# First modulation rows ahead of x, the first norm in wide tiles, and the order of the first products

## The chip, the cores and the metric

The kernel runs on one core of a Trainium2 chip (trn2). The metric is device time in microseconds (us), the median over runs of the same program. Engines are called TensorE (PE in the profile; PEld are its weight loads), VectorE (DVE), ScalarE (ACT), GpSimd (POOL) and SyncE (SP); SP issues most of the loads.

## The reference

One inference step of a two-layer diffusion backbone, all float32, for 512 latent and 128 prompt tokens of width 1024. What matters here is the beginning of layer 0:

```
def rms_norm(x, g):
    y = xf * lax.rsqrt(jnp.mean(xf * xf, axis=-1, keepdims=True) + RMS_EPS)
    return (y * g)

def ada_modulation(cond, w_mod, b_mod):
    m = jax.nn.silu(cond) @ w_mod + b_mod
    return jnp.split(m, 6, axis=-1)
...
        sh1_s, sc1_s, g1_s, sh2_s, sc2_s, g2_s = ada_modulation(cond_lat, w_mod[l], b_mod[l])
        hp = modulate(rms_norm(xp, norm_mix[l]), sh1_p, sc1_p)     # h * (1 + scale) + shift
        hs = modulate(rms_norm(xs, norm_mix[l]), sh1_s, sc1_s)
        # even layer: p = h @ w_in, split into latent attention, rotary key, neighbourhood attention
```

After it come two kinds of attention, output projection, a SwiGLU feed-forward layer, and layer 1 with grouped-query attention and its own feed-forward layer. The change touches only the first modulation, the first norm and the first projection.

## The kernel before

Activations lie with features on the 128 partitions: x is eight tiles `x[k]` of 128 features by 640 tokens, of which the first 512 are latent and the last 128 prompt tokens. Tokens are handled in two halves of 320 (`HALF`). Every float32 product is made of three: both operands are split into a high and a low part (`hh`, `hl` for activations, `unit` for weights: ScalarE makes the high part at L173, VectorE the low one at L174), and `mm3` issues high-high, high-low and low-high.

`Norm.add` (L201) squares a half tile on ScalarE and adds it to `acc` on VectorE; `Norm.rstd` (L211) sums over partitions with a product by ones on TensorE, and makes the reciprocal root with Ln and Exp on ScalarE, a half at a time (`n00p`, `n00rs` in the profile). `Mod.make` (L228) turns one half tile of x into `hh` and `hl`: VectorE multiplies by norm and scale (`h00t`, L234), ScalarE adds the shift (`h00h`, L238), VectorE makes the low part (`h00l`, L239). The second half has two conditions, so each step of it is two instructions (192 and 128 columns): a tile takes six on VectorE.

`mod0(j)` computes shift and scale for tiles 2j and 2j+1. Its two parts, called the rows of j, are 16 products of 32x256 each over one 1 MB load (`mraw`, fetched by `fetch`); ScalarE copies the sum out (`modsb`, L349), and `end` turns it with four small products by `sel`, and VectorE adds the bias (`mods`, L357). `mkgs` makes the scale column (`gs`, L364).

The stage is written out by hand. SP's queue issues x, the first rows' loads, wA0, the second rows' loads, wA1 and wA4, then the third and fourth rows' loads. `run(pieces)` has each piece begin after the last TensorE instruction issued before it, so TensorE's order is the written one; inside the pieces and on the other engines a planner orders the instructions, and each engine runs its own list in order. `first(ks, us)` issues the products of the activation tiles `ks` with the weight units `us`: unit 0 is wA0, units 1 and 2 are wA1 and wA4; two tiles and one unit are 12 products, with both other units 24. `made(j)` ends the modulation of j and makes tiles 2j and 2j+1. The order before is: the norm, rows 0, made(0), rows 1, 12 products of tiles 0 and 1 with wA0, made(1), 24 products with wA1 and wA4, rows 2, and so on with tiles 2 to 7. Behind the stage stand the products with wA2 and wA3 (`ckv0a`, from 53.3 us), and the rest of the kernel, whose text is the same in both versions.

Of the kernel before, what the change touches and what calls it, by code (L numbers as in the profile page):

```python
# [11 lines left out]
F32 = mybir.dt.float32  # L12
F32R = mybir.dt.float32r
AF = mybir.ActivationFunctionType
# [4 lines left out]
P = 128  # L19
D = 1024  # L20
KT = D // P
NS = 512
NP = 128
T = NS + NP
# [14 lines left out]
SH1, SC1, G1, SH2, SC2, G2 = 0, 8, 16, 24, 32, 40  # L39
# [12 lines left out]
def body(ctx, tc, xT, vecs, crow, wm0, wm0g1, wm0g, wm1, wA, wNV, wNA, wMK, wMV, wOA, wGQ, wGK, wGV, wOC,  # L52
         wFI, wFO, wFO1, cckvT, ckrT, cnkT, cnv, cgkT, cgv, rpbp, tabM, tabK, tabG, maskN,
         yT, o_ckvT, o_krT, o_nkT, o_nv, o_gkT, o_gv):
    nc = tc.nc
    V, S, G = nc.vector, nc.scalar, nc.gpsimd

    class PE:

        last = None  # L60
# [10 lines left out]
    ring = ctx.enter_context(tc.tile_pool(name="ring", bufs=8))  # L71
# [17 lines left out]
    def bank(name, kind="m"):  # L89
        if kind == "m":  # L90
            return psp.tile([P, 512], F32, tag="m", bufs=4, name=name)
        return ypool["pool"].tile([P, 512], F32, tag=kind, bufs=ypool["tags"][kind], name=name)
# [4 lines left out]
    def pair(name, kind="y"):  # L97
        return [bank(f"{name}a", kind), bank(f"{name}b", kind)]
# [7 lines left out]
    def f(ap):  # L106
        return ap.bitcast(F32)
# [4 lines left out]
    HALF = ((0, HT), (HT, T))  # L112
    HCOND = (((0, HT, 0),), ((HT, NS, 0), (NS, T, 1)))

    def run(pieces):

        for piece in pieces:
            with tc.issue_after(PE.last.ins):
                piece()
# [26 lines left out]
    mods = [main.tile([P, 48, 2], F32, name=f"mods{l}") for l in range(2)]  # L146
    gs = [[main.tile([P, 8, 2], F32, name=f"gs{l}{i}") for i in range(2)] for l in range(2)]
# [7 lines left out]
    def bc2(ap):  # L155
        return bass.AP(tensor=ap.tensor, offset=ap.offset, ap=list(ap.ap) + [[0, 2]])
# [6 lines left out]
    def load(src, n, name):  # L163
        raw = rawp.tile([P, 1024], F32, tag="raw", name=name)
        nc.sync.dma_start(raw[:, :n], src)
        return raw[:, :n]

    def unit(src, n, name, lo="v", pool=None, bufs=3):

        raw = load(src, n, name + "r")  # L170
        t = (pool or wp).tile([P, 2, 1024], F32R, tag="w", bufs=bufs, name=name)
        hi, lw = t[:, 0, :n], t[:, 1, :n]
        S.activation(hi, raw, AF.Copy)  # L173
        (V if lo == "v" else G).tensor_tensor(lw, raw, f(hi), ALU.subtract)  # L174
        return hi, lw
# [7 lines left out]
    def mm3(ps, a, b, h, l, st, sp, **k):  # L183
        PE.matmul(ps, a, h, start=st, stop=False, **k)
        PE.matmul(ps, a, l, start=False, stop=False, **k)
        PE.matmul(ps, b, h, start=False, stop=sp, **k)

    def proj(ps, wh, wl, hh, hl, ks, c0, c1, first=True, last=True, w0=0):

        for j, k in enumerate(ks):  # L190
            a, b = wh[:, (w0 + j) * P:(w0 + j + 1) * P], wl[:, (w0 + j) * P:(w0 + j + 1) * P]
            mm3(ps[:, :c1 - c0], a, b, hh[k][:, c0:c1], hl[k][:, c0:c1], first and j == 0, last and j == len(ks) - 1)


    class Norm:
# [5 lines left out]
        def add(self, x, i):  # L201
            c0, c1 = HALF[i]
            if self.k[i] == 0:
                S.activation(self.acc[:, c0:c1], x[:, c0:c1], AF.Square)
            else:
                sq = tp.tile([P, HT], F32, tag="u", bufs=7, name=f"{self.name}sq{self.k[i]}{i}")
                S.activation(sq, x[:, c0:c1], AF.Square)
                V.tensor_add(self.acc[:, c0:c1], self.acc[:, c0:c1], sq)
            self.k[i] += 1

        def rstd(self, i):  # L211
            c0, c1 = HALF[i]
# [118 lines left out]
    def mod0(j, bk, load_):  # L331

        box = []

        def part(half):
            def run():
                if half == 0:
                    box.append(bk())
                psm, rs = box[0], load_(j, half)

                for g in range(4):
                    for b in range(2):
                        o = 512 * (g % 2) + 256 * b
                        rows = slice(64 * b + 32 * (g % 2), 64 * b + 32 * (g % 2) + 32)
                        PE.matmul(psm[rows, :256], scol[:, 4 * half + g, :], rs[g // 2][:, o:o + 256], start=half == 0 and g < 2,
                                  stop=half == 1 and g > 1, tile_position=(0, rows.start))
                if half == 1:
                    box.append(tp.tile([P, HT], F32, tag="u", bufs=7, name=f"modsb{j}"))
                    S.activation(box[1][:, :256], psm[:, :256], AF.Copy)  # L349
            return run  # L350

        def end():
            psm, sb = box
            for i in range(2):
                PE.matmul(psm[:, 4 * i:4 * i + 4], sb[:, i * P:(i + 1) * P], sel, start=True, stop=True)
            for i, t in enumerate(MOD0[j]):
                V.tensor_tensor(mods[0][:, t:t + 2, :], psm[:, 0:8].rearrange("p (a i b) -> p a i b", a=2, b=2)[:, :, i, :],  # L357
                                bc2(bmod(0, t, 2)), ALU.add)
        return [part(0), part(1), end]

    def mkgs(l, i, k0=0, k1=8):
        sc = SC1 if i == 0 else SC2
        n = (V_NMIX if i == 0 else V_NFFN) + 8 * l
        V.scalar_tensor_tensor(gs[l][i][:, k0:k1, :], mods[l][:, sc + k0:sc + k1, :], 1.0, bc2(vec[:, n + k0:n + k1]),  # L364
                               ALU.add, ALU.mult)
# [111 lines left out]
        return get  # L477


    nrm = Norm("n00", D)  # L480
    x = []
    for k in range(KT):
        xk = ring.tile([P, T], F32, tag="x", name=f"x0_{k}")
        nc.sync.dma_start(xk, xT[:, k, :])
        x.append(xk)
    for k in range(KT):
        for i in range(2):
            nrm.add(x[k], i)
    hm = Mod("h00", x, gs[0][0], mods[0], SH1, (range(8), range(8)))
    hh, hl = hm.hh, hm.hl  # L490
    pss = [pair(f"wA{u}") for u in range(2)] + [[bank(f"wA2{c}") for c in range(2)]]

    def first(ks, us):
        for k in ks:
            for u in us:
                for c, (c0, c1) in enumerate(HALF):
                    proj(pss[u][c], *w3[u], hh, hl, [k], c0, c1, first=k == 0, last=k == KT - 1, w0=k)

    with tc.tile_pool(name="start", bufs=1) as big:
        raws = {}  # L500

        def fetch(j):
            for half in range(2):
                raws[j, half] = big.tile([P, 2, 1024], F32, tag="mraw", bufs=8, name=f"mraw{j}_{half}")
                nc.sync.dma_start(raws[j, half], wm0[j, 2 * half:2 * half + 2].rearrange("q p n -> p q n"))


        fetch(0)
        w3 = [unit(wA[0], 1024, "wA0")]
        fetch(1)  # L510
        w3 += [unit(wA[i], 1024, f"wA{i}") for i in (1, 4)]
        fetch(2)
        fetch(3)
        m = [mod0(j, lambda j=j: bank(f"mod{j}", "m"), lambda j, half: [raws[j, half][:, q, :] for q in range(2)]) for j in range(4)]

        def made(j):

            m[j][2]()
            mkgs(0, 0, 2 * j, 2 * j + 2)
            for k in (2 * j, 2 * j + 1):  # L520
                for i in range(2):
                    hm.make(i, nrm.rs, k)

        def rows(j):
            return m[j][:2]

        nrm.rstd(0)
        run([lambda: nrm.rstd(1)] + rows(0))
        run([lambda: made(0)] + rows(1))
        run([lambda: first((0, 1), [0]), lambda: made(1), lambda: first((0, 1), [1, 2])])  # L530
        run(rows(2))
        run([lambda: first((2, 3), [0]), lambda: made(2), lambda: first((2, 3), [1, 2])])
        run(rows(3))
        run([lambda: first((4, 5), [0]), lambda: made(3), lambda: first((4, 5), [1, 2])])
        run([lambda u=u: first((6, 7), [u]) for u in range(3)])
    sb = ExitStack()
# [53 lines left out]
    pss = [pair(f"ckv{u}") for u in range(2)]  # L590
# [15 lines left out]
    for kk in range(4):  # L606
# [3 lines left out]
        for j in range(2):  # L610
            k = 2 * kk + j
            a, b = wh[:, 512 * j:512 * (j + 1)], wl[:, 512 * j:512 * (j + 1)]
            for i in range(5):
                c0, c1 = P * i, P * i + P
# [256 lines left out]
    for h in range(8):  # L871
# [9 lines left out]
        qh, ql, ks = [t[r] for t in nqk[p]]  # L881
# [771 lines left out]
    x, pend = mixer_out(wOA, oMs + oNs, [4, 5, 6, 7, 0, 1, 2, 3], x_again, mods[0], "oa", nxt, op[-1], before(op[1], op[5], (1, 1, 1, 1, 0, 0, 0)))  # L1653
    box2, nxt = next_mod("h10", gs[1][0], mods[1], SH1)
    x, pend = ffn(0, x, pend, box["m"], nxt, side, op)


    hh, hl = box2["m"].hh, box2["m"].hl
# [17 lines left out]
    pss = [pair(f"gk{v}") for v in range(2)]  # L1676
# [165 lines left out]
    for h in range(8):  # L1842
# [4 lines left out]
        if h < 7:  # L1847
# [13 lines left out]
    x, pend = mixer_out(wOC, oGs, list(range(8)), lambda n, x=x: x[n], mods[1], "oc", nxt, op[-1],  # L1861
                        before(op[5], op[5], (2, 1, 1, 2, 1, 1, 0)), True)
# [9 lines left out]
    x, pend = ffn(1, x, pend, box["m"], final, lambda pool: lambda kind, i: None, op)  # L1872
# [158 lines left out]
```

## Time and profile before

| | |
|---|---|
| median of 3 runs | 1502.68 us (1501.55 to 1503.84) |
| the profiled execution | 1505.78 us |
| its span in the profile | 1503.8 us |
| TensorE busy, share of the span | 1449.1 us, 96% |
| VectorE, ScalarE, GpSimd busy | 82%, 52%, 12% |
| chain that ended last: TensorE, VectorE, DMA, ScalarE | 76%, 10%, 6%, 5% |
| loads from HBM | 193.15 MB |

The profile is one execution. The page cuts the span in 40 equal slices and gives each engine's busy share in tenths. A line of a timeline has start, length, engine, source line, operation, output <- inputs, shapes, and in brackets the idle time before it and what ended that. Several instructions of one kind are merged into one line (x4), whose length runs from the first start to the last end. For a load the last number of its line is the time from issue to landing.

### The profile page before, as it was taken

How to read it: one execution, taken by the hardware profiler on the slowest of the kernel's cores; microseconds unless marked ns; L12 is line 12 of the kernel's file. 1: busy time of each engine (PE TensorE's matmuls, PEld its weight loads, DVE VectorE, ACT ScalarE, POOL GpSimd, SP SyncE). 2: the span in 40 equal slices, each digit the busy share in tenths (PEclk: the TensorE clock that was granted, in tenths of full speed). 3: DMA queues.
4: the chain of work that ended last, by engine and by line, in shares of the span. 5: the costliest groups of instructions: out<-in, count | busy, mean ns of one | idle time of the engine just before them, and what ended most of it. 6: DMA issues, size and time to landing. Idle time of an engine off the chain costs nothing.

```text
span 1503.8 us, 25821 instructions
## 1 busy us (share of the span) xinstructions
PE 1449.1 (96%) x9762; PEld 1392.3 (93%) x9762; DVE 1234.7 (82%) x2378; ACT 784.8 (52%) x1535; POOL 175.5 (12%) x270
## 2 busy tenths in 40 slices
PE   5999989899999999999999999999999999999997
PEld 4989978889889999999999999989899999999996
DVE  5877778876878888965898887887899989889976
ACT  5446677763735555542123566673565555655442
POOL 0046636320000000000000122220100000000000
PEclk9999999999999999999999999999999999999998
DMA  9653341025154555549765301115245555548561
GB/s 370 206 152 121 113 144 43 15 85 183 38 198 152 171 171 171 165 165 348 233 224 171 102 33 32 41 42 184 69 156 169 191 173 191 175 155 293 185 257 70
DMA packets 79636, 231.48 MB, mean 154 GB/s; under 512 B 8857, under 2 KB 13241, under 8 KB 79129
## 3 DMA queue, kind: packets, MB, share of 16 engines
q1 hardware_dynamic: 77152, 225.43, 44.9%
q10 hardware_dynamic: 1944, 3.48, 0.7%
q8 instruction: 76, 1.25, 0.3%
q0 software_dynamic: 416, 0.93, 0.2%
q14 instruction: 48, 0.39, 0.1%
HBM read 193.15 MB, written 36.66 MB: 153 GB/s over the span
## 4 chain that ended last, share of the span: by engine, by line
PE 76%; DVE 10%; DMA 6%; ACT 5%; issue 2%; POOL 1%; SPq 0%; ACTq 0%; DVEq 0%; POOLq 0%
PE fg L64 19%; PE fd L64 8%; PE fgo L64 5%; PE fu L64 4%; PE gq L64 3%; PE fdo L64 2%; DVE junk L1602 2%; PE fo L64 2%; PE nk L64 2%; PE go L64 2%; PE gs L64 2%; PE nq L64 2%; DMA wm<-in_wm 1%; PE fuo L64 1%; DMA mraw<-in_wm 1%
## 5 line engine op out<-in xcount | busy, mean ns | idle before, releaser
L1602 DVE SCALAR_TENSOR_TENSOR junk<-wm,cb 128x1024 bf16<-128x1024 f32 x88 | 107.3, 1219 | 3.9 <-DMA wm<-in_wm 3.3
L64 PE MATMUL gq<-h10h,wgq 128*128 128x320 f32 x256 | 65.8, 316 | 0.0
L248 POOL TENSOR_SCALAR h10h<-h10t,gs,mods 128x320 fp32r<-128x320 f32 x4 | 3.1, 787 | 441.0 <-DVE h10t L242 438.6
L1342 ACT ACTIVATE wY<-s 128x1024 fp32r<-128x1024 f32 x37 | 39.2, 1060 | 27.7 <-PE fg L64 24.0
L1342 ACT ACTIVATE wZ<-s 128x1024 fp32r<-128x1024 f32 x37 | 39.1, 1057 | 17.8 <-PE fd L64 15.3
L1451 DVE TENSOR_TENSOR sg<-up,sg 128x640 f32<-128x640 f32 x37 | 30.4, 822 | 20.8 <-ACT sg L1450 20.3
L1343 DVE TENSOR_TENSOR wZ<-s,wZ 128x1024 fp32r<-128x1024 f32 x37 | 45.2, 1221 | 2.5 <-ACT wZ L1342 0.2
L64 PEld LDWEIGHTS gq<-h10h,wgq 128*128 128x128 f32 x256 | 44.9, 189 | 0.6
L1343 DVE TENSOR_TENSOR wY<-s,wY 128x1024 fp32r<-128x1024 f32 x37 | 45.1, 1218 | 0.3
L64 PE MATMUL fg<-h01q,wgu 128*128 128x320 f32 x192 | 40.8, 319 | 0.9 <-ACT h01q L285 0.5
L1450 ACT ACTIVATE sg<-fg 128x320 f32<-128x320 f32 x37 | 16.2, 438 | 48.7 <-PE fg L64 48.7
L1472 ACT ACTIVATE p<-fd 128x320 f32<-128x320 f32 x37 | 16.2, 438 | 46.7 <-PE fd L64 46.6
L1805 ACT ACTIVATE gp<-gs,gb,rq 128x640 f32<-128x640 f32 (+1 forms) x40 | 31.8, 795 | 15.3 <-DVE gb L1804 13.6
L64 PE MATMUL gq<-h10l,wgq 128*128 128x320 f32 x128 | 39.5, 309 | 0.0
L64 PE MATMUL fg<-h11q,wX 128*128 128x320 f32 x228 | 36.7, 309 | 0.0
L64 PE MATMUL fu<-h11q,wX 128*128 128x320 f32 x228 | 36.7, 309 | 0.0
L64 PE MATMUL fd<-h11q,wZ 128*128 128x320 f32 x228 | 36.6, 309 | 0.0
L64 PE MATMUL fg<-h11E,wW 128*128 128x320 f32 x228 | 36.5, 309 | 0.0
L64 PE MATMUL fg<-h11N,wZ 128*128 128x320 f32 x228 | 36.5, 309 | 0.0
L64 PE MATMUL fd<-h11D,wY 128*128 128x320 f32 x228 | 36.4, 308 | 0.0
L64 PE MATMUL fg<-h11C,wY 128*128 128x320 f32 x228 | 36.4, 308 | 0.0
L64 PE MATMUL fg<-h01E,wW 128*128 128x320 f32 x216 | 34.7, 310 | 0.4 <-DVE g L1482 0.4
(3387 smaller groups left out, 5289.7 us busy)
## 6 DMA issues: line engine op xcount, KB each, us to landing
wm<-in_wm SPq DMA_DIRECT2D x48, 512.0 KB, 4.4
mraw<-in_wm SPq DMA_DIRECT2D x8, 1024.0 KB, 13.1
mraw<-in_wm SPq DMA_DIRECT2D x16, 512.0 KB, 3.7
wmv<-in_wm0g SPq DMA_DIRECT2D x8, 512.0 KB, 4.1
wm<-in_wm0g SPq DMA_DIRECT2D x8, 512.0 KB, 5.5
ruo<-in_wFO SPq DMA_DIRECT2D x8, 512.0 KB, 3.9
rgo<-in_wFO SPq DMA_DIRECT2D x8, 512.0 KB, 5.5
x<-in_xT SPq DMA_DIRECT2D x8, 320.0 KB, 5.7
```

The costliest lines, as they stand in the source:

```text
L64: cls.last = nc.tensor.matmul(*a, **k)
L248: G.tensor_scalar(h[:, c0:c1], t, self.gsl[:, k, 0:1], self.ml[:, self.sh + k, 0:1], ALU.mult, ALU.add)
L1342: S.activation(h, src, AF.Copy)
L1343: V.tensor_tensor(w_, src, f(h), ALU.subtract)
L1450: last = S.activation(sg[:, 0:HT], g[:, :HT], AF.Silu, scale=-1.0)
L1451: V.tensor_tensor(sg, up, sg, ALU.mult)
L1472: S.activation(p5, b5[:, :HT], AF.Copy)
L1602: V.scalar_tensor_tensor(junk, raw, 1.0, cb[:, c, :], ALU.mult, ALU.mult, accum_out=mods[l][:, j0 + i, c:c + 1])
L1805: S.activation(dst, src, AF.Exp, bias=nb, scale=rq[:, j:j + 1], accum_out=ll[:, j:j + 1])
```

## The change

The two loads of the first rows are issued ahead of the eight loads of x. The rows of j = 0, their end and their scale column come ahead of the norm. The new `Norm.both` squares and adds whole tiles of 640 columns, and takes only the last tile in halves; the wide squares use a buffer of the tag `hl` instead of `u`. `made(0)` no longer ends a modulation. The second rows come behind the 12 products of tiles 0 and 1 with wA0, where they stood ahead of them. Rows 2 and 3 keep their places.

```diff
+        def both(self, x, apart):
+            if self.k[0] == 0:
+                S.activation(self.acc, x, AF.Square)
+            elif apart:
+                for i in range(2):
+                    self.add(x, i)
+                return
+            else:
+                sq = ring.tile([P, T], F32, tag="hl", name=f"{self.name}sq{self.k[0]}")
+                S.activation(sq, x, AF.Square)
+                V.tensor_add(self.acc, self.acc, sq)
+            self.k = [self.k[0] + 1] * 2
...
-    nrm = Norm("n00", D)
-    x = []
-    for k in range(KT):
-        xk = ring.tile([P, T], F32, tag="x", name=f"x0_{k}")
-        nc.sync.dma_start(xk, xT[:, k, :])
-        x.append(xk)
-    for k in range(KT):
-        for i in range(2):
-            nrm.add(x[k], i)
...
         fetch(0)
+        nrm = Norm("n00", D)
+        x = []
+        for k in range(KT):
+            xk = ring.tile([P, T], F32, tag="x", name=f"x0_{k}")
+            nc.sync.dma_start(xk, xT[:, k, :])
+            x.append(xk)
...
+        def ready(j):
+            m[j][2]()
+            mkgs(0, 0, 2 * j, 2 * j + 2)
+
+        run(rows(0) + [lambda: ready(0)])
+        for k in range(KT):
+            nrm.both(x[k], k == KT - 1)
         w3 = [unit(wA[0], 1024, "wA0")]
         fetch(1)
...
         def made(j):
 
-            m[j][2]()
-            mkgs(0, 0, 2 * j, 2 * j + 2)
+            if j:
+                ready(j)
             for k in (2 * j, 2 * j + 1):
                 for i in range(2):
                     hm.make(i, nrm.rs, k)
...
         nrm.rstd(0)
-        run([lambda: nrm.rstd(1)] + rows(0))
-        run([lambda: made(0)] + rows(1))
-        run([lambda: first((0, 1), [0]), lambda: made(1), lambda: first((0, 1), [1, 2])])
-        run(rows(2))
-        run([lambda: first((2, 3), [0]), lambda: made(2), lambda: first((2, 3), [1, 2])])
-        run(rows(3))
+        run([lambda: nrm.rstd(1)])
+        made(0)
+        w3 += [unit(wA[i], 1024, f"wA{i}") for i in (1, 4)]
+        fetch(2)
+        fetch(3)
+        run([lambda: first((0, 1), [0])] + rows(1))
+        run([lambda: made(1), lambda: first((0, 1), [1, 2])] + rows(2))
+        run([lambda: first((2, 3), [0]), lambda: made(2), lambda: first((2, 3), [1, 2])] + rows(3))
         run([lambda: first((4, 5), [0]), lambda: made(3), lambda: first((4, 5), [1, 2])])
         run([lambda u=u: first((6, 7), [u]) for u in range(3)])
```

More of the change, by code (lines that the diff above doesn't have):

```diff
@@ L477, in lazy @@
         return get
-    nrm = Norm("n00", D)
-    x = []
-    for k in range(KT):
-        xk = ring.tile([P, T], F32, tag="x", name=f"x0_{k}")
-        nc.sync.dma_start(xk, xT[:, k, :])
-        x.append(xk)
-    for k in range(KT):
-        for i in range(2):
-            nrm.add(x[k], i)
[L489 to L497, printed above, removed]
     with tc.tile_pool(name="start", bufs=1) as big:
@@ L508, in body, with rows, first, made @@
         fetch(0)
+        nrm = Norm("n00", D)
[4 more added lines that the diff above has]
+            x.append(xk)
+        m = [mod0(j, lambda j=j: bank(f"mod{j}", "m"), lambda j, half: [raws[j, half][:, q, :] for q in range(2)]) for j in range(4)]
+        def rows(j):
+            return m[j][:2]
+        def ready(j):
[4 more added lines that the diff above has]
+            nrm.both(x[k], k == KT - 1)
         w3 = [unit(wA[0], 1024, "wA0")]
         fetch(1)
+        hm = Mod("h00", x, gs[0][0], mods[0], SH1, (range(8), range(8)))
+        hh, hl = hm.hh, hm.hl
+        pss = [pair(f"wA{u}") for u in range(2)] + [[bank(f"wA2{c}") for c in range(2)]]
+        def first(ks, us):
+            for k in ks:
+                for u in us:
+                    for c, (c0, c1) in enumerate(HALF):
+                        proj(pss[u][c], *w3[u], hh, hl, [k], c0, c1, first=k == 0, last=k == KT - 1, w0=k)
+        def made(j):
+            if j:
+                ready(j)
+            for k in (2 * j, 2 * j + 1):
+                for i in range(2):
+                    hm.make(i, nrm.rs, k)
+        nrm.rstd(0)
+        run([lambda: nrm.rstd(1)])
+        made(0)
         w3 += [unit(wA[i], 1024, f"wA{i}") for i in (1, 4)]
@@ L513, in body @@
         fetch(3)
-        m = [mod0(j, lambda j=j: bank(f"mod{j}", "m"), lambda j, half: [raws[j, half][:, q, :] for q in range(2)]) for j in range(4)]
-        def made(j):
-            m[j][2]()
-            mkgs(0, 0, 2 * j, 2 * j + 2)
[L520 to L527, printed above, removed]
-        run([lambda: nrm.rstd(1)] + rows(0))
-        run([lambda: made(0)] + rows(1))
-        run([lambda: first((0, 1), [0]), lambda: made(1), lambda: first((0, 1), [1, 2])])
-        run(rows(2))
-        run([lambda: first((2, 3), [0]), lambda: made(2), lambda: first((2, 3), [1, 2])])
-        run(rows(3))
+        run([lambda: first((0, 1), [0])] + rows(1))
+        run([lambda: made(1), lambda: first((0, 1), [1, 2])] + rows(2))
+        run([lambda: first((2, 3), [0]), lambda: made(2), lambda: first((2, 3), [1, 2])] + rows(3))
         run([lambda: first((4, 5), [0]), lambda: made(3), lambda: first((4, 5), [1, 2])])
```

## The prediction

> **What bounds the kernel now.** I read the 40 slices of the page first, then the chain of waits from the start, then the table of stretches and the timeline of each engine up to 54 us.
>
> ```profile
> PE   5999989899999999999999999999999999999997
> 4.31 5.72 DMA x<-in_xT
> 10.05 13.13 DMA mraw<-in_wm
> 23.23 1.93 PE mod L64 x16
> 9.00:10.00 1.00, 0.00 (x0) 0.00 (x0) 0.99 (x3) 1.00 (x3) 0.00 (x0) 1.00 1.03 410
> 53.30:110.00 56.70, 56.70 (x317) 51.36 (x317) 48.04 (x83) 23.31 (x44) 16.18 (x30) 1.00 0.60 183
> ```
>
> The first slice is the only low one before the last: 37.6 us in which TensorE is half idle. The three lines of the chain (start, length, what) say that its critical part is loading: x, then the modulation rows until 23.18 us, and only then TensorE. The stretch from 9 to 10 us shows the DMA engines full (share 1.03, 410 GB/s). After 53.3 us TensorE is busy through the stretch (56.70 of 56.70 us), so a delay of the first projection's end goes to the end of the kernel nearly whole. The order of instructions on every engine, compared between the two programs, differs only in this first stage. So the question is one number: when the 24 products that follow the second rows are done. Before, they end where the third rows begin, at 32.05 us (row below).
>
> **Transfers.** The change issues the two transfers of the first rows (L505, 2 MB) ahead of the eight of x (L484) on SP's queue; wA0, the second rows and all later ones keep their places.
>
> ```profile
> 4.31 1.30 SPq L484 DMA_DIRECT2D x<-in_xT  x3
> 5.66 1.76 SPq L505 DMA_DIRECT2D mraw<-in_wm  x2
> 8.37 0.34 SPq L165 DMA_DIRECT2D wA0r<-in_wA  x1
> x<-in_xT SPq DMA_DIRECT2D x1, 320.0 KB, 6.5
> mraw<-in_wm SPq DMA_DIRECT2D x1, 1024.0 KB, 9.7
> wA0r<-in_wA SPq DMA_DIRECT2D x1, 512.0 KB, 9.7
> 5.00:6.00 1.00, 0.20 (x1) 0.00 (x0) 0.00 (x0) 0.99 (x2) 0.00 (x0) 1.00 0.93 268
> 6.00:7.00 1.00, 0.00 (x0) 0.00 (x0) 0.00 (x0) 1.00 (x4) 0.00 (x0) 1.00 0.92 241
> ```
>
> The last x is issued at about 5.2 us and lands 6.5 later, at 11.7. The second half of the first rows is issued at about 6.9 and lands 9.7 later, at 16.6. Swapped, the same bytes lie ahead of the last x as lay ahead of that half, so x ends at 16.6, 4.9 us later; wA0 lands at 18.07 (8.37 + 9.7) in both. Where this could be off: the rate fell to 268 and 241 GB/s from 5 to 7 us. Without that dip some 0.3 MB more come in, 0.75 us at 410 GB/s: x at 15.85 at best. I take 16.6, since nothing says that the dip goes.
>
> **The norm.** Before, 16 squares of 320 columns and 14 additions kept ScalarE and VectorE behind the loads. Now each tile is 640 wide, except the last, which stays in halves, and x comes at the loads' pace, so only the last half counts.
>
> ```profile
> L207 ACT ACTIVATE n00sq<-x x14: 452/454/470, 6.6 to 12.3; 128x320 f32<-128x320 f32 x14
> L208 DVE TENSOR_TENSOR n00acc<-n00acc,n00sq x14: 470/473/493, 7.1 to 13.4; 128x320 f32<-128x320 f32 x14
> 13.50 2.50 PE L64 MATMUL n00p<-n00acc,ones 128*128 128x320 f32 x4 [8.30 <-DVE n00acc L208]
> 14.97 0.53 ACT L215 ACTIVATE n00rs<-n00p,eps 128x320 f32<-128x320 f32 x1 [2.21 <-PE n00p L64]
> 15.53 0.47 ACT L216 ACTIVATE n00rs<-n00rs 128x320 f32<-128x320 f32 x1
> 18.77 1.05 ACT L173 ACTIVATE wA<-wA0r 128x1024 fp32r<-128x1024 f32 x1
> ```
>
> One square (0.454) and one addition (0.473) after 16.6 put the first half's sum at 17.55. TensorE's two sums take 2.50 from there, to 20.05. ScalarE first makes the high part of wA0, which lands at 18.07 (1.05, to 19.12), then Ln and Exp of the first half to 19.7, and those of the second, after TensorE's 20.05, by 21.1 (0.53 + 0.47 and a gap). The 640-wide tiles take seven squares and six additions off each queue, worth nothing here: that work lies under the loads. If two 640-wide operations ran behind the loads, the cost would be one operation, under 1 us.
>
> **VectorE's part.** After the norm VectorE makes the first two tiles, 12 operations (made(0)); half 1 of the first tile waits for the 21.1 above, and everything behind it in VectorE's queue waits too.
>
> ```profile
> 20.09 0.88 DVE L234 SCALAR_TENSOR_TENSOR h00t<-x,gs,n00rs 128x320 f32<-128x320 f32 x2
> 24.40 1.14 DVE L239 SCALAR_TENSOR_TENSOR h00l<-h00t,mods,h00h 128x320 fp32r<-128x320 f32 x3
> 36.85 1.61 DVE L234 SCALAR_TENSOR_TENSOR h00t<-x,gs,n00rs 128x320 f32<-128x320 f32 x4
> 40.83 0.68 DVE L239 SCALAR_TENSOR_TENSOR h00l<-h00t,mods,h00h 128x192 fp32r<-128x192 f32 x2 [0.26 <-ACT h00h L238]
> ```
>
> Before, these ran from 20.09 to 25.54, with wA0's low part among them. Undisturbed, such a dozen takes 36.85 to 41.51 less the 0.26 of idle time, 4.4 us. One of the twelve (0.47) runs ahead of 21.1, so 3.95 are left: 25.05. wA0's low part now lies ahead of them, under the wait for the norm. So the two tiles are ready only 0.5 us earlier than before: what the early first rows save, the late x takes away. This is the heart of the forecast.
>
> **TensorE's part.** The order becomes: first rows and norm, 12 products with wA0, second rows, their four small products, 24 products with wA1 and wA4. Before, the second rows lay ahead of the 12, under VectorE's work.
>
> ```profile
> 18.92 0.61 PE L64 MATMUL mod<-sel,modsb 128*128 128x4 f32 x4 [0.51 <-ACT modsb L349]
> 20.76 1.94 PE L64 MATMUL mod<-mraw,scol 128*32 128x256 f32 x16 [1.23 <-DMA mraw<-in_wm]
> 25.09 0.64 PE L64 MATMUL wA0a<-h00h,wA 128*128 128x320 f32 x1
> 25.53 0.47 PE L64 MATMUL wA0a<-h00l,wA 128*128 128x320 f32 x1
> 25.79 0.47 PE L64 MATMUL wA0a<-h00h,wA 128*128 128x320 f32 x1
> 27.96 0.50 PE L64 MATMUL mod<-sel,modsb 128*128 128x4 f32 x4
> 28.32 0.39 PE L64 MATMUL wA1a<-h00h,wA 128*128 128x320 f32 x1
> 32.05 1.93 PE L64 MATMUL mod<-mraw,scol 128*32 128x256 f32 x32
> ```
>
> The 12 products now start near 22 us (before 25.09), at VectorE's pace; the last two come after 25.05 at 0.27 each (25.53 to 25.79), so they end at 25.6. The second rows landed at 23.2 and wait for nothing: 32 products, 0.12 us each at half clock (16 in 1.94), 0.06 at full (32 in 1.93). Then ScalarE copies their result out while TensorE stands, 0.51 us as at 18.92; before, the 12 products covered that, and that cover is gone. The small products take 0.36 (27.96 to 28.32), the 24 products 3.73 (28.32 to 32.05). Low parts of wA1 and wA4 keep up: VectorE is free from 25.05 for wA1 (24.5 us is its landing), and wA4's comes behind the second modulation as before.
>
> The clock decides between 0.12 and 0.06.
>
> ```profile
> 17.10:20.51 3.41, 1.92 (x28) 1.00 (x20) 0.81 (x4) 1.33 (x2) 0.00 (x0) 1.00 1.02 408
> 20.51:23.93 3.42, 2.64 (x24) 1.09 (x28) 3.42 (x9) 1.58 (x4) 0.00 (x0) 0.50 1.03 411
> 23.93:27.34 3.41, 3.41 (x20) 2.45 (x13) 2.35 (x6) 3.15 (x6) 0.00 (x0) 0.50 1.03 408
> 293.58:296.99 3.41, 1.71 (x12) 1.15 (x10) 3.32 (x8) 2.81 (x9) 0.93 (x2) 1.00 0.00 0
> 296.99:300.40 3.41, 2.86 (x11) 2.67 (x12) 2.04 (x6) 1.05 (x3) 0.37 (x1) 0.50 0.00 0
> 440.35:443.76 3.41, 3.41 (x15) 3.41 (x14) 3.38 (x5) 0.05 (x1) 0.00 (x0) 0.50 0.97 298
> ```
>
> The columns are the stretch, its length, the busy time of TensorE, its weight loads, VectorE, ScalarE and GpSimd, and the granted clock. The clock changes on steps of 3.41 us: a step with TensorE busy 1.92 or 1.71 us is followed by half clock, one at half clock with 2.64 stays there, and ones with 2.86 or 3.41 bring full clock back. In the changed kernel TensorE is busy 3.2 of 3.6 us from 22 on (12 x 0.267), so a step can count from about 22 to 25.4; full clock comes between 25.4 and 28.9. I take 27.3, where it came before: 14 row products at half clock (1.7) and 18 at full (1.1) end at 28.4, the copy at 28.9, the small products at 29.25, the 24 products at 33.0. Against 32.05 that is **+0.9 us**. Bounds: full clock from 25.6 on gives 25.6 + 1.93 + 0.51 + 0.36 + 3.73 = 32.1, +0.1; half clock through rows and small products (3.87, 0.51, 0.61) gives 34.3, +2.3. With the dip gone 0.75 comes off each, so this band is -0.65 to +2.3.
>
> By the Trainium skill, page "TensorE: Matmul & The Clock Gate", section "What's actually happening", the window is 3.4 us long, runs freely, and one busy window of sustained work releases the clock; the length agrees with the 3.41 us here. Taken strictly, so that only an unbroken window counts, it would have to lie behind about 25.1 us, and the switch would come from 28.5 on, the sum near +2.0 and the time near 1504.7. The step from 296.99, busy for only 2.86 us, speaks against that strictness.
>
> **After this stage.** The third rows were waited for by nobody at 32.05, and they keep their place in the queue, so they are there at 33.0. VectorE's second dozen ends 0.75 us later than before, still under those rows and the products behind them. The rest is the same order with TensorE bound: +0.9 carries. The profiled run took 1505.78 us (span 1503.8), which would become 1506.7; on the median, 1502.68, it is **1503.6 us**. A difference of 0.2%, 3.0 us, is about what a measurement of this kernel can tell from no change.
>
> **Rivals.**
> *Slower: half clock holds through the 24 products.* The stand of 0.51 us for the copy, together with VectorE's pace before it, could keep two steps in a row below what the clock asks for. Then rows, copy and small products end at 30.6 and the 24 products take 24 x 0.267 = 6.4 us: 37.0, +4.9, 1507.6 us. It is over 0.2% if half clock lasts beyond 32.3 us. For it: a step busy 2.64 of 3.42 us stayed at half clock. Against it: one with 2.86 did not. Chance 0.26.
> *Faster: the clock gains elsewhere.* Two later steps at half clock, from 296.99 and 440.35, follow idle spots of TensorE. If the moved start sets the 3.41 us steps so that these spots are shared between two steps, both drops go, worth half of 2.86 and of 3.41 us, 3.1 us; with the dip gone (0.75) and full clock early (+0.1) the sum is -3.8, 1498.9 us. Against it: nothing binds the steps to the change, so runs of both kernels should draw alike. Chance 0.18.
> *The change does nothing here:* if x lost less than 4.9 us, because transfers of one queue overlap more than I read, each microsecond would come off directly until the second rows' landing at 23.2 binds; the time would be 1502 to 1503, inside "same".
>
> **Numbers.** Forecast and the do-nothing case, within 0.2%: 0.56. The range, 1499.4 to 1507.3, takes the band of -0.65 to +2.3 with some 1 us for what runs differ by, and reaches half way into either rival.
>
> **What would show it.** Right: last x landing near 16.6 and n00p near 17.6 us; TensorE's first wA0 product near 22 with gaps on VectorE; second rows after 25 us; an idle 0.5 us before their small products; third rows at 33. Wrong: x landing before 14, third rows starting before 31 or after 35, or a difference that arises behind 54 us.

## The result, and the profile after

The changed kernel takes 1505.1 us (median of 22 runs, 1501.84 to 1508.93) against 1502.36 for the kernel before (22 runs, 1496.41 to 1506.07): the ratio is 1.0018, 95% interval 1.001 to 1.0026, or 2.7 us more. It is slower, by just under the 0.2% that the prediction called measurable, and inside its range.

The two profiled executions alone would say the opposite: the span after is 1501.3 us, before 1503.8. The profile of after has no stretch at half clock between 29.4 and 1493.7 us, that of before has two (from 296.99 and from 440.35 us, rows in the prediction). Such stretches come and go from run to run: a second profile of the changed kernel has two of them (from 202.00 and from 300.99 us). They also go with the time: of the 22 runs, the five with a mean granted clock of 0.993 or less have a median of 1506.77 us, the six with 0.997 or more 1503.48. The change has therefore to be read in its stage. These are TensorE's lines there, from the timeline of the changed kernel (start, length, what, idle time before it):

```profile
6.46 1.93 PE L64 MATMUL mod<-mraw,scol 128*32 128x256 f32 x16 [1.19 <-DMA mraw<-in_wm]
9.23 1.94 PE L64 MATMUL mod<-mraw,scol 128*32 128x256 f32 x16 [0.84 <-DMA mraw<-in_wm]
18.36 2.50 PE L64 MATMUL n00p<-n00acc,ones 128*128 128x320 f32 x4 [5.43 <-DVE n00acc L208]
22.43 0.64 PE L64 MATMUL wA0a<-h00h,wA 128*128 128x320 f32 x1 [1.57 <-ACT h00h L251]
25.39 0.63 PE L64 MATMUL wA0a<-h00l,wA 128*128 128x320 f32 x1
25.82 0.47 PE L64 MATMUL wA0a<-h00h,wA 128*128 128x320 f32 x1
26.62 0.47 PE L64 MATMUL wA0b<-h00h,wA 128*128 128x320 f32 x1
27.02 3.07 PE L64 MATMUL mod<-mraw,scol 128*32 128x256 f32 x32
30.61 0.61 PE L64 MATMUL mod<-sel,modsb 128*128 128x4 f32 x4 [0.52 <-ACT modsb L362]
31.07 0.40 PE L64 MATMUL wA1a<-h00h,wA 128*128 128x320 f32 x1
34.91 1.93 PE L64 MATMUL mod<-mraw,scol 128*32 128x256 f32 x32
```

The first rows run at 6.46 and 9.23 us, out of everybody's way. The first product with wA0 starts at 22.43, 2.7 us earlier than before, but the 12 products give way to the second rows only at 27.02. Then come the second rows, with nobody else's work to hide them, the stand of 0.52 us for ScalarE's copy, the small products and the 24 others. The third rows begin at 34.91 us; before they began at 32.05. These 2.86 us agree with the 2.7 us of the medians, and they are carried on whole: the first product behind the stage starts 2.87 us later than before (first row from the timeline of the kernel before, second from that of the changed one).

```profile
53.13 0.31 PE L64 MATMUL ckv0a<-h00h,wA 128*128 128x320 f32 x1
56.00 0.31 PE L64 MATMUL ckv0a<-h00h,wA 128*128 128x320 f32 x1
```

From 53 us on TensorE is again busy through the stretch. The timeline of ScalarE and VectorE in the changed kernel shows why the early first rows bring nothing; the last row is the stretch from 53 to 110 us by windows (length, busy time and count of TensorE, its weight loads, VectorE, ScalarE and GpSimd, then granted clock, DMA share and GB/s):

```profile
15.82 0.83 ACT L207 ACTIVATE n00sq<-x 128x320 f32<-128x320 f32 x2
21.45 0.47 ACT L229 ACTIVATE n00rs<-n00rs 128x320 f32<-128x320 f32 x1
13.02 0.23 DVE L370 TENSOR_TENSOR mods<-mod,vec 128x4 f32<-128x4 f32 x2 [0.58 <-PE mod L64]
14.09 3.61 DVE L221 TENSOR_TENSOR n00acc<-n00acc,n00sq 128x640 f32<-128x640 f32 x4
17.81 0.89 DVE L208 TENSOR_TENSOR n00acc<-n00acc,n00sq 128x320 f32<-128x320 f32 x2
24.78 1.15 DVE L252 SCALAR_TENSOR_TENSOR h00l<-h00t,mods,h00h 128x320 fp32r<-128x320 f32 x3
53.00:110.00 57.00, 57.00 (x322) 51.66 (x321) 48.49 (x81) 25.59 (x49) 13.73 (x26) 1.00 0.56 173
```

The modulation is ready at 13 us, but the norm only at 21.92 (21.45 + 0.47), and tiles 0 and 1 at 25.93 (24.78 + 1.15) against 25.54 before.

### The profile page after: what moved, and what is told of

The parts are those of the page before. It is cut to its first block, busy times and chain, and to the rows that moved or that the text cites. A ratio compares the mean times of both kernels' runs of the same rounds, so it can differ in the third digit from the quotient of the medians.

```text
span 1501.3 us, 25799 instructions
## 1 busy us (share of the span) xinstructions
PE 1448.8 (97%) x9762; PEld 1390.4 (93%) x9762; DVE 1233.6 (82%) x2372; ACT 782.6 (52%) x1528; POOL 175.6 (12%) x270
```

## The experiments

Theory A, the prediction's own: the second rows have lost their cover. Rivals: B, the late x and norm cost the time; C, the difference comes from the clock later in the run.

**Second rows ahead again**, all else as changed.

```diff
-        run([lambda: first((0, 1), [0])] + rows(1))
+        run(rows(1) + [lambda: first((0, 1), [0])])
```

> The changed kernel with one thing undone: the second rows stand ahead of the 12 products with wA0 again, everything else as changed (first rows and their loads ahead of x, wide norm). Theory A (the second rows lost their cover: VectorE's making of tiles 0 and 1 used to hide them): they run from their landing (20.6 to 23.2 us) to about 25.1, the 12 products end near 28.3 and the third rows begin near 32.4 us, as before the change (32.05) and 2.5 earlier than changed (34.91); the time is within 1 us of the kernel before. Theory B (the late x and norm cost the time): tiles 0 and 1 are still ready at 25.9, third rows still begin near 34.5, time +2.5 us. Theory C (the +2.7 us come from the clock later in the run): no change of the stage and a time that differs by chance only.

1502.88 us, ratio to before 1.0006 (0.9995 to 1.0017). Its timeline, TensorE and then VectorE's last step of tiles 0 and 1:

```profile
21.47 2.64 PE L64 MATMUL mod<-mraw,scol 128*32 128x256 f32 x32
24.04 0.42 PE L64 MATMUL wA0a<-h00h,wA 128*128 128x320 f32 x1
26.92 0.31 PE L64 MATMUL wA0b<-h00h,wA 128*128 128x320 f32 x1
31.73 1.93 PE L64 MATMUL mod<-mraw,scol 128*32 128x256 f32 x32
25.47 1.14 DVE L252 SCALAR_TENSOR_TENSOR h00l<-h00t,mods,h00h 128x320 fp32r<-128x320 f32 x3
```

The rows now run while VectorE makes the tiles. The third rows begin at 31.73 us, and no loss can be told from zero, although the tiles are ready even later here (26.61). That is A, and against B: the late x alone shows no cost. It is against C too: when the stage got its 3.2 us back, the median fell by 2.2.

**Second rows behind, in the kernel before**, all else as before.

```diff
-        run([lambda: made(0)] + rows(1))
-        run([lambda: first((0, 1), [0]), lambda: made(1), lambda: first((0, 1), [1, 2])])
+        run([lambda: made(0), lambda: first((0, 1), [0])] + rows(1))
+        run([lambda: made(1), lambda: first((0, 1), [1, 2])])
```

> The kernel before with one thing done: the second rows stand behind the 12 products with wA0; loads, norm and first rows as before. Theory A: the products run at VectorE's pace from about 21.3 to 26.3, the second rows to 29.4, the copy and the small products to 30.4, third rows near 34.2 us (before 32.05): +2.1 us. Theory B: third rows stay near 32, time within 0.5 us of before. Theory C: the same as B.

1505.7 us, ratio 1.0018 (1.0003 to 1.0032): this one move alone costs as much as the whole change. TensorE in its timeline:

```profile
21.80 0.63 PE L64 MATMUL wA0a<-h00h,wA 128*128 128x320 f32 x1 [1.76 <-ACT h00h L238]
26.73 0.47 PE L64 MATMUL wA0b<-h00h,wA 128*128 128x320 f32 x1
27.13 2.52 PE L64 MATMUL mod<-mraw,scol 128*32 128x256 f32 x32
34.33 1.93 PE L64 MATMUL mod<-mraw,scol 128*32 128x256 f32 x32
```

**Filler products for the clock**, in the kernel before and in the changed one.

```diff
+        def filler(n, a, cols):
+            for _ in range(n):
+                PE.matmul(pss[0][0][:, :cols], ones, a[:, :cols], start=True, stop=True)
...  before:
-        nrm.rstd(0)
+        run([lambda k=k: filler(1, x[k], 448) for k in range(KT)] + [lambda: nrm.rstd(0)])
-        run([lambda: made(0)] + rows(1))
+        run([lambda: made(0), lambda: filler(3, x[0], HT), rows(1)[0], lambda: filler(2, x[0], HT), rows(1)[1]])
...  changed: filler(1, x[k], HT) likewise, filler(2, x[0], HT) behind rstd(1), and among the 12 products
+                        if k < 2 and ks[0] == 0 and us == [0] and (k, c) != (1, 1):
+                            for _ in range(2):
+                                PE.matmul(pss[1][0][:, :P], ones, f(hh[k][:, c0:c0 + P]), start=True, stop=True)
```

> The kernel before with 13 filler products on TensorE (ones times parts of x into a bank that is overwritten later), one per landed tile of x and five around the first of the second rows, to keep its clock up; the results do not use them. Theory A with the clock as its second cause (half clock from 20.5 to 27.3 us costs rows and products twice their time): full clock from about 13 us on, second rows end near 24.2 instead of 25.16, the 12 products near 26.0 instead of 27.96, and the third rows begin near 30.8 instead of 32.05: -1.3 us, 1501. If the clock costs nothing there because VectorE and the loads set the pace, third rows stay at 32 and the time is the same or up to 1 us longer by the fillers.

> The changed kernel with 16 filler products: one per landed tile of x, two behind the norm's sums, six among the 12 products, so that TensorE's clock is full by about 18 us and stays so. Theory A with the clock as its second cause: norm 0.5 us earlier, 12 products end near 25.7 instead of 27.0, second rows 1.93 instead of 3.07 us, third rows near 32.1 instead of 34.91: the time equals that of the kernel before within 0.5 us. If only the order counts and not the clock, third rows stay near 34.5 and the time at +2.5 us.

Both missed. The first took 1503.91 us, ratio 1.0009 (0.9996 to 1.0023), third rows at 32.68; the second 1506.96, ratio 1.0033 (1.0021 to 1.0045), third rows at 34.44. Two lines of TensorE from the timeline of the second:

```profile
20.44 1.24 PE L64 MATMUL n00p<-n00acc,ones 128*128 128x320 f32 x4
27.84 1.93 PE L64 MATMUL mod<-mraw,scol 128*32 128x256 f32 x32
```

The clock did what was wanted: the norm's sums take 1.24 instead of 2.50 us and the second rows 1.93 instead of 3.07. But VectorE's last addition had ended at 19.10 us, and the fillers stood in TensorE's queue until 20.44, so the norm's sums began that late (18.36 in the changed kernel); the first product with wA0 came at 23.84 instead of 22.43, and the gain was used up. In the kernel before, three fillers took 3.02 us ahead of the second rows, most of it at half clock (from 20.34 us). Whether a full clock without such a price would win is left open by these two.

**The norm's width**, alone in the kernel before, and taken back in the changed one.

```diff
-        for i in range(2):
-            nrm.add(x[k], i)
+        nrm.both(x[k], k == KT - 1)
```

> The kernel before with the wide norm alone (loads, rows and products in the order of before). If wide additions are the slower way (each waits for the one before it on the same sum: four took 3.61 us in the changed kernel, 0.93 each when in a row, against 0.41 for a half), the norm's first sum comes no earlier than before (13.5 us) though x has landed at 11.7, and since the first rows land at 16.6 anyway, the third rows begin at 32.0 to 32.6 us: time within 0.5 us of before. If wide tiles help, the sum comes near 12.8 us and the third rows still begin near 32, because the first rows' landing binds: also the same time. The trace tells the two apart, the time does not.

> The changed kernel with the norm in halves as before, all else as changed. If the wide additions and the modulation between them hold VectorE behind the loads: the norm's first sum near 17.3 us instead of 18.4, tiles 0 and 1 ready near 25.0 instead of 25.9, third rows near 33.9 instead of 34.9 us: about -1 us against the changed kernel, +1.7 against before. If the load sets the norm's time: 18.4 and 34.9 again, +2.7 us.

Wide alone: 1501.96 us, ratio 1.0003 (0.9988 to 1.0017), third rows at 32.12; the norm's first sum comes 0.9 us later than before (14.36 against 13.50), as four wide additions take 3.61 us here too. The time shows no cost. In the stage a small one is not excluded: tiles 0 and 1 are ready at 27.00 us instead of 25.54, and the third rows begin as before, but here with full clock from 19.18 us on; the kernel before, with full clock from 17.35 us in its second profile, began them at 31.05. Narrow in the changed kernel: 1505.51 us, ratio 1.0029 (1.0018 to 1.0039), third rows at 34.86. That expectation failed, as its timeline shows (VectorE, then TensorE):

```profile
13.32 0.23 DVE L370 TENSOR_TENSOR mods<-mod,vec 128x4 f32<-128x4 f32 x2 [7.67 <-PE mod L64]
13.94 5.31 DVE L208 TENSOR_TENSOR n00acc<-n00acc,n00sq 128x320 f32<-128x320 f32 x13
18.90 2.50 PE L64 MATMUL n00p<-n00acc,ones 128*128 128x320 f32 x4 [5.68 <-DVE n00acc L208]
```

The end of the first modulation now stands ahead of all additions in VectorE's queue and waits for TensorE until 13.32, so the additions start late and still end late: from the first square to the sum it is 8.29 us (10.61 to 18.90) against 8.33 with wide tiles (10.03 to 18.36). Width is not what counts there.

**The modulation's end behind the additions.**

```diff
-        run(rows(0) + [lambda: ready(0)])
+        run(rows(0))
         for k in range(KT):
             nrm.both(x[k], k == KT - 1)
+        after(nrm.last, lambda: ready(0))
...  in Norm.add, so that nrm.last is the last addition:
-                V.tensor_add(self.acc[:, c0:c1], self.acc[:, c0:c1], sq)
+                self.last = V.tensor_add(self.acc[:, c0:c1], self.acc[:, c0:c1], sq)
```

> The changed kernel with the end of the first modulation (VectorE's two mods and one gs) issued behind the norm's additions instead of between them. If those three short operations push the additions back: first sum 0.5 to 0.8 us earlier (17.6 to 17.9), third rows near 34.2. If the additions' own chain is what is slow: first sum 0.0 to 0.3 us earlier and third rows at 34.6 to 34.9, time +2.5 us against before.

1504.31 us, ratio 1.002 (1.001 to 1.0031), third rows at 33.75. Its timeline, ScalarE, VectorE and TensorE:

```profile
10.66 0.74 ACT L213 ACTIVATE n00acc<-x 128x640 f32<-128x640 f32 x1 [4.69 <-DMA x<-in_xT]
12.26 5.47 DVE L221 TENSOR_TENSOR n00acc<-n00acc,n00sq 128x640 f32<-128x640 f32 x6 [6.51 <-ACT n00sq L220]
18.38 2.50 PE L64 MATMUL n00p<-n00acc,ones 128*128 128x320 f32 x4 [4.82 <-DVE n00acc L208]
27.03 1.93 PE L64 MATMUL mod<-mraw,scol 128*32 128x256 f32 x32
```

The sum did not come at 17.6 to 17.9 us, as expected, since x landed 0.6 us later in this run. From the first square to the sum it is 7.72 us (10.66 to 18.38), in the changed kernel 8.33 (10.03 to 18.36). The second profile of the changed kernel, in which x landed at the same moment as here, agrees: 10.63 to 18.96, again 8.33. So the three short operations cost 0.6 us. The third rows gain 1.2 us on the first profile of the changed kernel because the clock was full when the second rows began (1.93 us). The time is not told apart from that of the changed kernel.

**Only the early first rows are left**: narrow norm and second rows ahead.

> The changed kernel with the norm in halves and the second rows ahead of the 12 products again: only the first rows and their loads ahead of x are left of the change. Theory A: norm near 17.3 us, second rows right behind its sums (landed by 22 to 23.2), tiles 0 and 1 ready near 25.0, third rows near 31.0 us instead of 32.05 before: 1501.2 us, 1 us faster than the kernel before. Theory B (the late x costs more than the early rows bring): third rows at 32.5 or later, time at or above that of before.

1502.48 us, ratio 1.0001 (0.9989 to 1.0013), third rows at 31.80. The norm's sum came at 19.11 us, not 17.3: as in the narrow kernel above, the additions stood behind the modulation's end until 13.52 us. There is no gain to be measured, and no version here is told apart from the kernel before as faster.

**Half the rows, and both kernels once more.**

```diff
-        run([lambda: first((0, 1), [0])] + rows(1))
+        run([rows(1)[0], lambda: first((0, 1), [0]), rows(1)[1]])
```

> The changed kernel with the second rows split: their first 16 products (landed by about 21 us) ahead of the 12 products with wA0, the other 16 behind them. Theory A (what counts is how much of the second rows lies uncovered behind VectorE's tiles 0 and 1): half the loss, the third rows begin between 32.8 and 33.6 us, +1.2 us against the kernel before. If the copy and the small products behind the rows (0.5 and 0.4 to 0.6 us) are the larger part of the loss, it stays above 34 us.

> The changed kernel unchanged, for a second profile of it. If the moment at which TensorE's clock becomes full sets the size of the loss (26.95, 28.38, 29.00 and 29.38 us went with third rows at 33.75, 34.33, 34.86 and 34.91 in four kernels with the second rows behind), this run's pair lies on the same line, about 0.5 us per microsecond; if not, the third rows begin at 34.9 whatever the clock does.

> The kernel before unchanged, for a second profile. With the second rows under VectorE's work the clock's moment should matter little: third rows between 31.6 and 32.7 us wherever full clock falls between 19 and 30 us; a value over 33 would mean that the first profile of it was a lucky one and the loss smaller than 2.9 us.

Split: 1503.64 us, ratio 1.0008 (0.9996 to 1.0021), third rows at 34.12. That is not half the loss (32.8 to 33.6), but above 34, as the second reading had it. It does not settle the matter: the clock, full at 23.03 us, fell to half at 26.44, and the 16 row products left behind took 1.94 us, about as long as 32 at full clock; the time lies between. The changed kernel again: ratio 1.0019 (1.0009 to 1.0029), third rows at 34.47 with full clock at 27.92, some 0.3 us above the line through the other four, since its norm's sum came 0.6 us later than in the first profile. So the clock's moment counts, but not alone. The kernel before again: ratio 1.0 (0.9991 to 1.001), third rows at 31.05, outside the 31.6 to 32.7 expected: its clock was full from 17.35 us, and 16 of its row products took 1.07 us, as its timeline of TensorE shows:

```profile
22.63 1.07 PE L64 MATMUL mod<-mraw,scol 128*32 128x256 f32 x16 [1.39 <-DMA mraw<-in_wm]
31.05 1.93 PE L64 MATMUL mod<-mraw,scol 128*32 128x256 f32 x32
```

The profiles side by side, by where the second rows stand (us; full clock is the last change to full clock ahead of the third rows):

| kernel | full clock | second rows end | third rows begin |
|---|---|---|---|
| before | 27.34 | 25.16 | 32.05 |
| before, again | 17.35 | 23.70 | 31.05 |
| wide only | 19.18 | 23.87 | 32.12 |
| rows ahead | 22.96 | 24.11 | 31.73 |
| narrow, rows ahead | 23.54 | 24.43 | 31.80 |
| changed | 29.38 | 30.09 | 34.91 |
| changed, again | 27.92 | 29.67 | 34.47 |
| before, rows behind | 28.38 | 29.65 | 34.33 |
| narrow, changed | 29.00 | 30.18 | 34.86 |
| modulation's end late | 26.95 | 28.96 | 33.75 |

The two groups do not meet, whatever norm and load order they have. With the rows behind, the third rows begin 4.7 to 4.8 us after the second rows end in all five: everything between is a fixed chain of copy, small and 24 products, so whatever delays the rows' end delays the third rows by as much. With the rows ahead, that distance ranges from 6.9 to 8.3 us, and the rows' own end does not set it.

## Why the prediction was right, and where its size was off

**Loads.** Predicted: last x at 16.6 us, 15.85 if the dip went. Its squares begin at 15.82 in the changed kernel's first profile, and near 16.5 in others (16.51 with the rows ahead, 16.45 with the modulation's end late). Right, and both cases occur.

**The norm.** The largest error is here. "Only the last half counts" allowed 0.95 us from x's landing to the first sum; it took 2.54 (15.82 to 18.36), 1.6 us more, of which x's landing 0.8 us before 16.6 gave half back. VectorE was behind the loads: in the rows above, additions to one sum follow each other at 0.93 us, while the squares of x come every 0.8, and the modulation's end cost 0.6. The prediction had named this case and capped it at one operation; it is nearly two. So tiles 0 and 1 were ready at 25.93, not 25.05: 0.88 us.

**The 12 products.** Predicted to end 0.55 us behind VectorE, they ended 1.09 behind it: the last four products, behind the 25.39 line (25.82 to 26.62), run in a row at 0.27 us, half clock, and they, not VectorE, set the end: 0.54 us.

**Second rows, copy, small products, 24 products.** All as told, with the stand of 0.52 us (0.51 predicted). Full clock came at 29.38, outside the 25.4 to 28.9 given, so the rows took 3.07 instead of 2.8 us; 0.1 each for the small and the 24 products. Together: 0.88 + 0.54 + 0.27 + 0.2 = 1.9 us, which is the difference between +0.9 and +2.86. The sign and the place were right, and the mechanism is shown in both directions by the first two experiments; the terms of TensorE's wait were too small.

**The clock.** "Full clock between 25.4 and 28.9" held in three of the five profiles with the rows behind (26.95, 27.92, 28.38) and failed in two (29.00, 29.38). The reading below it, that a step from about 22 to 25.4 us could count since steps busy for 2.86 us had brought full clock back, failed in the changed kernel. These are its two steps before the switch:

```profile
22.55:25.96 3.41, 3.32 (x9) 2.32 (x10) 3.34 (x10) 2.38 (x6) 0.00 (x0) 1.00 1.03 408
25.96:29.38 3.42, 3.42 (x29) 1.91 (x31) 1.22 (x1) 0.37 (x1) 0.00 (x0) 1.00 1.03 411
```

The clock column shows 1.00 here, but the products run at 0.27 us each, as they did before at a granted clock of 0.50. In the first step TensorE was busy for 3.32 of 3.41 us, and full clock still came only after the next one, busy without a break. In all five profiles the step ahead of the switch was busy without a break, as the strict reading of the prediction asks; three switches came before its 28.5 us because those steps began earlier than assumed (23.53, 24.51 and 24.97 us instead of 25.1).

The Trainium skill, page "TensorE: Matmul & The Clock Gate", section "What's actually happening", has one busy window of sustained work release the clock. Other steps of these traces fit no strict form of that: 2.86 us busy were enough from 296.99 us in the kernel before, 3.02 from 26.44 in the split kernel, and in the second profile of the changed kernel a step busy without a break (202.00 to 205.41) was followed by another at half clock. What a step must hold stays open.

**The rivals.** Half clock through the 24 products did not happen in any profile. The faster rival's clock gain happened in the first profiled run of the changed kernel (no half clock later on, span 2.5 us shorter), not in the second and, as its own counterargument said, not in the median. That x loses clearly less than 4.9 us by overlap fell: it lost 4.1 to 4.8 (landing at 15.82 to 16.5 instead of 11.7), between the two values that the bytes gave.

## What to carry to other kernels

Before moving work of a waiting engine behind something "to start that earlier", ask what will fill the wait that it filled: here 32 products that were hidden under VectorE's work cost the kernel 2.7 us once they stood behind it. Moving one chain's data ahead of another's on a full queue exchanged which chain was late. When a change is worth less than the spread that the clock gives single runs, compare the moment at which its stage ends over several profiles, not the span of two.

## What the runs showed of the hardware that was not expected

Single runs of one program differ by up to 10 us (1496.41 to 1506.07 for the kernel before), more than the change is worth, and the time goes with the granted clock: of 90 further runs of the kernel before, the 13 with a mean of 0.991 or less have a median of 1505.2 us, the 35 with 0.995 or more 1500.54. In one profile of it the clock was full from 17.10 us, half from 20.51 and full again from 27.34; in the other it stayed full from 17.35.

How busy TensorE is in a step does not tell when full clock is lost. The split kernel lost it at 26.44 us after a step busy for 2.52 of 3.41 us; the kernel before kept it in its second profile through one busy for 2.02 (20.76 to 24.17).
